# First four gate/up tile pairs by eight plain products on the first two token blocks; input loads and norm reordered

## The chip, the cores and the metric

The kernel runs on one core of one Trainium2 chip. TensorE (PE, with its weight loads PEld) does the matrix products, VectorE (DVE), ScalarE (ACT) and GpSimd (POOL) the elementwise work, and SyncE (SP) issues the DMAs. The metric is the device time of one execution in microseconds (us). TensorE's clock is granted at one of two levels, 1.2 or 2.4 GHz; the profile gives the granted share (1.00 is 2.4 GHz).

## The reference, cut to what matters

One decoder layer on 1104 token rows (16 meta rows, 1024 of the prompt, 64 of the samples) of width 1024, with a feed-forward block (FFN) ahead of the token mixers and one behind them:

```
x = x + 0.5*swiglu(rmsnorm(x, ffn1_norm), ffn1_w_gu, ffn1_w_down)
...                                   # input projection, four mixers, merge, output projection
x = x + 0.5*swiglu(rmsnorm(x, ffn2_norm), ffn2_w_gu, ffn2_w_down)
y = rmsnorm(x, final_norm)
def swiglu(x, w_gu, w_down):
    gate, up = split(x @ w_gu, 2, axis=-1)        # each 1104 x 2816
    return (silu(gate) * up) @ w_down
```

## The kernel before

Activations lie transposed: partitions are channels, columns are tokens. Each fp32 operand is split (`split`, L97 to L99) into a high part by an ACT cast and a low part by a DVE subtraction; a product of two split operands is three matmuls per 128 rows of depth.

**Gate and up** (`gate_up`, L411). The 2816 hidden columns are 22 tiles `f`. A pair is the gate tile and the up tile of one `f`. The tokens are four blocks of NS = 276; `p` = 0 is blocks 0 and 1, `p` = 1 is blocks 2 and 3. A pair on one `p` is a 2 by 2 by 2 block product (gate/up, two halves of the depth, two token blocks) done with seven products in place of eight (`steps`, L424). A product is 12 matmuls of 276 columns. The seven need sums of weight tiles (`a_prep`, L386: two raw tiles r1 and r2, a third raw tile s23, then casts) and sums of activation blocks, the factors B[p][0] to B[p][6] (`b_prep`, L363, with `factor`, L357). `two(0)` does `f` = 0 and 1 on `p` = 0; then `second()` loads the other half of the tokens and makes the factors of `p` = 1; `f` = 2 to 21 run on both `p`; `two(1)` does `f` = 0 and 1 on `p` = 1 at the end. The result goes by DMA to hS.

**Start of the first FFN** (`first`, `second`, `load_x`, L276). `load_x` loads row tiles of x (10 in all; 4, 2, 2 and 2 at a time), transposes them on TensorE (L67), copies them out with ACT (L309) and DVE (L307) in turn, takes the row sums of squares with ACT (L319) and DVE (L316) in turn, makes diagonal tiles on POOL (L326) and a matmul of them that spreads the norm over partitions (rs, L330). `scale` (L351) multiplies by norm and gain.

**Start of the second FFN.** `w_out` (the mixers' output projection) ends with the norm of each block; the same factors follow.

**Down** (`down`, L498). h is read back in groups of `f`: (2 to 5), (6 to 9), (10 to 13), (14 to 17), (18 to 21), then (0, 1). For each output tile `m` and token third `tb` (368 columns) a group adds into x by DVE (L511). The last group runs `tb` by `tb`, so that what follows a third, `norms` (L109) in the first FFN and `final` (L540) in the second, can begin beside the other thirds.

**Buffers that count.** wp holds 2 raw tiles and 3 each of whi and wlo; gw 2 raw tiles and 2 each; the pools up and v hold 8 and 6 slots. u22, block 3's second half (and its sums), lies in a raw tile of gw. The order on each engine is planned at build time: ready instructions go by priority, `high_priority` ahead of the rest, then by program order. Every DMA is issued by SP, in that order.

Of the kernel before, what the change touches and what calls it, by code (L numbers as in the profile page):

```python
# [7 lines left out]
F32 = mybir.dt.float32  # L8
# [5 lines left out]
D = 1024  # L14
DFF = 2816
# [27 lines left out]
class Kernel:  # L43
# [53 lines left out]
    def split(self, hi, lo, x):  # L97
        self.nc.scalar.copy(out=hi, in_=x)  # L98
        self.nc.vector.tensor_tensor(out=lo, in0=x, in1=hi.bitcast(F32), op=SUB)  # L99
# [176 lines left out]
    def load_x(self, half, xs):  # L276

        nc, I = self.nc, self.I
# [3 lines left out]
        blocks.append((I["x_sample"].rearrange("b t d -> (b t) d"), TS, TP))  # L282
        for pn, part in enumerate(((blocks[:4], blocks[4:6]), (blocks[6:8], blocks[8:]))[half]):
            ts = []
            for i, (src, r, c0) in enumerate(part):
                if i % 2 == 0:
                    pool = self.v if half and pn else self.up
                    xin = self.slot(pool, "xin", F32, (2, D))
                t = xin[:, i % 2]
                ld = nc.sync.dma_start(out=t[:r], in_=src).ins  # L290
                ts.append(t)
                if c0 == NMETA:
                    self.prm, self.po = self.gains()()
            self.after_x = ld
            for t, (src, r, c0) in zip(ts, part):
                for h in range(2):
                    ps = self.psum([128, 4, 128], "P" if h else "mm")
                    for j in range(4):
                        k = 4 * h + j
                        self.transpose(ps[:, j, :r], t[:r, k * 128:k * 128 + 128], r)  # L300
                    for b in range(c0 // NS, (c0 + r - 1) // NS + 1):
                        if b not in xs:
                            xs[b] = self.slot(self.v, "xs", F32, (8, NS))
                        lo, hi = max(c0, NS * b), min(c0 + r, NS * (b + 1))
                        dst, src = xs[b][:, 4 * h:4 * h + 4, lo - NS * b:hi - NS * b], ps[:, :, lo - c0:hi - c0]
                        if h:
                            nc.vector.tensor_copy(out=dst, in_=src)  # L307
                        else:
                            nc.scalar.copy(out=dst, in_=src)  # L309

            st = self.tp.tile([128, 3, 4], F32, tag="f_s", name="x_s")
            m, y, tmp = (st[:, i] for i in range(3))
            nc.gpsimd.memset(m, 0.0)
            for i, (t, (src, r, c0)) in enumerate(zip(ts, part)):
                if i % 2:
                    nc.vector.scalar_tensor_tensor(out=t[:r], in0=t[:r], scalar=1.0, in1=t[:r], op0=MULT, op1=MULT,  # L316
                                                   accum_out=m[:r, i:i + 1])
                else:
                    nc.scalar.activation(out=t[:r], in_=t[:r], func=AF.Square, accum_out=m[:r, i:i + 1])  # L319
            nc.vector.tensor_scalar(out=m, in0=m, scalar1=1.0 / D, scalar2=None, op0=MULT)  # L320
            self.rsqrt_rows(m, y, tmp)
            b0, n = part[0][2], 0
            ps = self.psum([128, 400], "P")
            for i, (src, r, c0) in enumerate(part):
                dg = self.tp.tile([128, 128], F32, tag="f_h", name="xdg")
                nc.gpsimd.tensor_scalar(out=dg[:r, :r], in0=self.ident[:r, :r], scalar1=y[:r, i:i + 1], scalar2=float(D),  # L326
                                        op0=MULT, op1=MULT)
                self.mm(ps[:, n:n + r], self.onesD[:r], dg[:r, :r])
                n += r
            nc.scalar.copy(out=self.rs[:, b0:b0 + n], in_=ps[:, :n])  # L330
        for b in (2 * half, 2 * half + 1):
            self.dq.dma_start(out=self.xS[:, :, NS * b:NS * (b + 1)], in_=xs[b])
# [24 lines left out]
    def factor(self, p, i, pool, x):  # L357

        t = self.slot(pool, f"b{p}{i}", F32R, (2, 4, NS))
        self.split(t[:, 0], t[:, 1], x)  # L360
        self.B[p][i] = t[:, 0], t[:, 1]

    def b_prep(self, p, u1, u2, u22, tmp, homes, first=0):  # L363


        tt = self.nc.vector.tensor_tensor
        b11, b21, b12, b22 = u1[:, 0:4], u1[:, 4:8], u2[:, 0:4], u22
        s3, s2 = tmp[:, 0:4], tmp[:, 4:8]
        if first == 0:
            self.factor(p, 0, homes[0], b11)  # L370
        self.factor(p, 1, homes[1], b21)
        tt(out=s3, in0=b22, in1=b12, op=SUB)
        tt(out=s2, in0=s3, in1=b11, op=ADD)
        tt(out=b12, in0=b12, in1=b11, op=SUB)
        self.factor(p, 2, homes[2], s2)
        self.nc.gpsimd.tensor_tensor(out=b21, in0=b21, in1=s2, op=SUB)
        self.factor(p, 4, homes[4], s3)
        if p:
            self.factor(p, 5, homes[5], b21)
            self.factor(p, 3, homes[3], b12)  # L380
        else:
            self.factor(p, 3, homes[3], b12)
            self.factor(p, 5, homes[5], b21)
        self.factor(p, 6, homes[6], b22)

    def a_prep(self, w, f):  # L386

        nc = self.nc
        with self.tc.high_priority() if f > 1 else ExitStack():
# [21 lines left out]
    def gate_up(self, w_in, first, second):  # L411
# [12 lines left out]
        def steps(f, A, p, q):  # L424
# [3 lines left out]
                 for c, pool, tag, n in (("a", self.ev, "e_a", 3), ("b", self.ev, "e_a", 3), ("c", self.tp, "f_s", 2),  # L428
# [42 lines left out]
        def two(p):  # L471
            run(*(steps(i, A, p, i) for i, A in enumerate([self.a_prep(w, i) for i in range(2)])))
        with self.tc.high_priority():
            first()
        two(0)
        second()
        for f in range(2, NF):
            a = self.a_prep(w, f)
            run(*(steps(f, a, p, p) for p in range(2)))
        yield  # L480
        two(1)

    GROUPS = [list(range(i, j)) for i, j in ((2, 6), (6, 10), (10, 14), (14, 18), (18, 22), (0, 2))]

    def load_h(self, fs):

        hs = []
        for f in fs:
            t = self.slot(self.v if fs == self.GROUPS[-1] else self.up, "h")
# [8 lines left out]
    def down(self, wd_in, start, hook=None, after=None):  # L498
# [6 lines left out]
        def out(hs, w, c0, m, tb):  # L505
            sl = slice(tb * NB, (tb + 1) * NB)
            o = m * 128 - c0
            ps = self.psum([128, NB])
            for i, (hh, hl) in enumerate(hs):
                self.mm3(ps, (w[0][:, i, o:o + 128], w[1][:, i, o:o + 128]), (hh[:, sl], hl[:, sl]), i == 0, i == len(hs) - 1)  # L510
# [4 lines left out]
        for gi, fs in enumerate(groups):  # L515
            hs = nxt
            cw = 1024 // len(fs)
            ws = []
            for c in range(1024 // cw):
# [1484 lines left out]
```

## Time and profile before

| what | before |
|---|---|
| median of 3 runs (2685.52 to 2690.02) | 2687.84 us |
| profiled execution | 2691.09 us |
| its span, first to last instruction | 2689.5 us |
| TensorE busy | 2528.3 us (94%), 17378 matmuls |
| VectorE busy | 1471.3 us (55%) |
| ScalarE busy | 913.8 us (34%) |
| mean granted clock | 0.968 |

The profiled execution is 1.6 us longer than its span and 3.25 us longer than the median. The busy shares are means over stages with different limits, so they say little of one stage; the windows of the section of rows below do.

### The profile page before, as it was taken

The page shows a single profiled execution, that of the slowest core. Times are in us where ns is not written, and L with a number is a line of the kernel's source. Part 1 is how long each engine was busy: PE and PEld are TensorE (multiplying, and loading weights), DVE is VectorE, ACT ScalarE, POOL GpSimd, SP SyncE. Part 2 cuts the span into 40 slices and gives each one's busy share as a digit, 9 for nine tenths or more (in the row PEclk, how much of TensorE's full clock was granted, in tenths as well). Part 3 has the DMA queues.
Part 4 walks back from the last instruction along what each step waited for, and adds up shares of the span by engine and source line. Part 5 has one row for each costly group of instructions (what it writes and reads, how often), then busy time and mean ns, then how long its engine had stood idle before and what let it go on. Part 6 is the DMA issues. An engine that isn't in the chain of part 4 may idle for free. (4 is left out here: it accounts for less than half of the span.)

```text
span 2689.5 us, 43298 instructions
## 1 busy us (share of the span) xinstructions
PE 2528.3 (94%) x17378; PEld 2452.0 (91%) x17378; DVE 1471.3 (55%) x2762; ACT 913.8 (34%) x1654; POOL 544.9 (20%) x595
## 2 busy tenths in 40 slices
PE   5599999999998988989999999999699999999997
PEld 5599999999997877978988999999699999999997
DVE  6644444556777448858653435343954444454535
ACT  4433333432204336324532313132433333341203
POOL 2122222200003003023452222212222222210000
PEclk7799999999998999989999999999899999999998
DMA  5222222453323232543443435332132222362311
GB/s 161 72 87 83 74 73 73 131 176 112 121 55 111 79 80 59 153 124 94 116 141 99 162 118 170 120 131 96 35 91 86 73 73 73 98 216 81 108 40 67
DMA packets 308997, 276.45 MB, mean 103 GB/s; under 512 B 62419, under 2 KB 266573, under 8 KB 308661
## 3 DMA queue, kind: packets, MB, share of 16 engines
q1 hardware_dynamic: 308797, 273.70, 32.9%
q8 instruction: 136, 2.23, 0.3%
q14 instruction: 64, 0.52, 0.1%
HBM read 192.11 MB, written 81.72 MB: 102 GB/s over the span
## 5 line engine op out<-in xcount | busy, mean ns | idle before, releaser
L59 PE MATMUL ps_mm<-u,whi 128*128 128x368 f32 (+1 forms) x2816 | 720.5, 337 | 11.4 <-DVE c_gl L144 4.7
L59 PE MATMUL ps_mm<-h,whi 128*128 128x368 f32 x2112 | 529.8, 332 | 3.3 <-DVE x L511 3.1
L59 PEld LDWEIGHTS ps_mm<-u,whi 128*128 128x128 f32 x2816 | 505.5, 191 | 26.9 <-issue 5.5
L98 ACT CAST whi<-raw 128x1024 fp32r<-128x1024 f32 (+1 forms) x303 | 297.7, 985 | 614.0 <-PE ps_mm L59 420.4
L59 PE MATMUL ps_mm<-u,wlo 128*128 128x368 f32 (+1 forms) x1408 | 471.7, 335 | 0.0
L59 PE MATMUL ps_mm<-b,whi 128*128 128x276 f32 x2816 | 446.8, 292 | 19.2 <-ACT b L98 10.0
L99 DVE TENSOR_TENSOR wlo<-raw,whi 128x1024 fp32r<-128x1024 f32 (+1 forms) x303 | 376.5, 1246 | 119.4 <-ACT whi L98 118.7
L59 PEld LDWEIGHTS ps_mm<-b,whi 128*128 128x128 f32 x2816 | 394.3, 190 | 21.5 <-ACT b L98 10.6
L59 PEld LDWEIGHTS ps_mm<-h,whi 128*128 128x128 f32 x2112 | 374.7, 188 | 6.6 <-DVE x L511 5.4
L59 PE MATMUL ps_mm<-h,wlo 128*128 128x368 f32 x1056 | 350.3, 332 | 0.0
L59 PEld LDWEIGHTS ps_mm<-u,wlo 128*128 128x128 f32 x1408 | 268.8, 191 | 4.2 <-issue 2.3
L511 DVE SCALAR_TENSOR_TENSOR x<-ps_mm,x 128x368 f32<-128x368 f32 x288 | 154.8, 539 | 187.3 <-PE ps_mm L59 185.8
L59 PE MATMUL ps_mm<-b,wlo 128*128 128x276 f32 x1408 | 237.5, 291 | 0.5 <-DVE wlo L99 0.5
L59 PEld LDWEIGHTS ps_mm<-b,wlo 128*128 128x128 f32 x1408 | 201.5, 189 | 0.8 <-DVE wlo L99 0.8
L59 PEld LDWEIGHTS ps_mm<-h,wlo 128*128 128x128 f32 x1056 | 198.4, 188 | 0.2
L401 POOL TENSOR_TENSOR raw<-raw 128x512 f32<-128x512 f32 x48 | 65.3, 1361 | 607.5 <-DVE wlo L99 570.4
L144 DVE TENSOR_TENSOR g_sg<-ps_mm,rs 128x368 f32<-128x368 f32 x96 | 51.8, 540 | 207.8 <-PE ps_mm L59 207.7
L59 PE MATMUL ps_vn<-b,whi 128*128 128x276 f32 x704 | 121.8, 294 | 36.5 <-ACT whi L98 36.5
L59 PEld LDWEIGHTS ps_vn<-b,whi 128*128 128x128 f32 x704 | 102.9, 192 | 37.0 <-ACT whi L98 36.9
L462 POOL TENSOR_TENSOR e_g<-e_g,e_u 128x276 f32<-128x276 f32 x88 | 105.3, 1197 | 109.6 <-ACT e_g L461 64.8
L439 DVE TENSOR_TENSOR e_g<-ps_pre,e_a 128x276 f32<-128x276 f32 x88 | 38.9, 442 | 156.5 <-DMA hS<-e_g 149.7
L59 PE MATMUL ps_o<-b,whi 128*128 128x276 f32 x704 | 120.1, 293 | 2.1 <-DVE e_u L452 2.1
(473 smaller groups left out, 3338.8 us busy)
## 6 DMA issues: line engine op xcount, KB each, us to landing
raw<-in_ffn_w_gu SPq DMA_DIRECT2D x96, 512.0 KB
raw<-in_w_in SPq DMA_DIRECT2D x50, 512.0 KB
hS<-e_g SPq DMA_DIRECT2D x88, 276.0 KB
h<-hS SPq DMA_DIRECT2D x44, 552.0 KB
raw<-in_ffn_w_down SPq DMA_DIRECT2D x44, 512.0 KB
x<-xS SPq DMA_DIRECT2D x24, 552.0 KB
mgS<-g_mg SPq DMA_DIRECT2D x24, 552.0 KB
g_b<-brS SPq DMA_DIRECT2D x16, 552.0 KB
```

Of the source, the lines that this page charges most:

```text
L59: self.last_mm = self.nc.tensor.matmul(out=out, lhsT=lhsT, rhs=rhs, start=start, stop=stop, **kw).ins
L98: self.nc.scalar.copy(out=hi, in_=x)
L99: self.nc.vector.tensor_tensor(out=lo, in0=x, in1=hi.bitcast(F32), op=SUB)
L144: self.last_dve = self.nc.vector.tensor_tensor(out=out, in0=ps, in1=r, op=MULT).ins
L401: nc.gpsimd.tensor_tensor(out=s23[:, k2], in0=r1[:, k1], in1=r2[:, k1], op=SUB)
L439: add(out=g[:, 0], in0=gam, in1=e["a"], op=ADD)
L462: nc.gpsimd.tensor_tensor(out=g[:, 1], in0=g[:, 1], in1=e["u"], op=MULT)
L511: nc.vector.scalar_tensor_tensor(out=x[:, m, sl], in0=ps, scalar=0.5, in1=x[:, m, sl], op0=MULT, op1=ADD)
```

## The change

The first four pairs (NP = 4) are no longer done by seven products on `p` = 0. `plain` does them by eight, one token block `t` at a time: on block 0 with B[0][0] and B[0][1] (the plain halves of that block), on block 1 with B[0][3] (the difference of the blocks' first halves, added to the kept sums e_a) and B[0][6] (block 1's second half); these are factors that the seven products use later. Their weights are only cast, not summed (`a_load`, `a_parts`). Pairs 0 and 1 run on block 0, then on block 1; pairs 2 and 3 likewise. `b_prep` is cut in two, `b_first` and `b_rest`. On `p` = 0 one subtraction of `b_rest` moves from DVE to POOL. `seven((0, 1), 1)` runs after `f` = 7, `seven((2, 3), 1)` at the end. In the first FFN all ten tiles of x are issued early, weights between them; `load_x` is cut into `load_x`, `turn_x` and `stats_x`; four tiles are copied out by ACT alone; all squares but one are on ACT; the diagonal tiles are made by ACT. The last group of `down` has three `f` in place of two, each with its own weight tile of 1024 columns.

```diff
+    def stats_x(self, ts, pool, tag):
...
+            if i == 1 and c0 < NS:
+                nc.vector.scalar_tensor_tensor(out=sq, in0=t[:r], scalar=1.0, in1=t[:r], op0=MULT, op1=MULT,
+                                               accum_out=m[:r, i:i + 1])
+            else:
+                nc.scalar.activation(out=sq, in_=t[:r], func=AF.Square, accum_out=m[:r, i:i + 1])
...
+            nc.scalar.activation(out=dg[:r, :r], in_=self.ident[:r, :r], func=AF.Copy, scale=y[:r, i:i + 1])
+            self.mm(ps[:, n:n + r], self.onesD[:r], dg[:r, :r])
...
-    def b_prep(self, p, u1, u2, u22, tmp, homes, first=0):
...
+    def b_first(self, p, u1, u2, u22, tmp, homes, skip=()):
+        for i, x in ((0, u1[:, 0:4]), (1, u1[:, 4:8])):
+            if i not in skip:
+                self.factor(p, i, homes[i], x)
+        self.nc.vector.tensor_tensor(out=tmp[:, 0:4], in0=u2[:, 0:4], in1=u1[:, 0:4], op=SUB)
+        self.factor(p, 3, homes[3], tmp[:, 0:4])
+        if p == 0:
+            self.factor(p, 6, homes[6], u22)
+    def b_rest(self, p, u1, u2, u22, tmp, homes):
+        b11, b21, b12 = u1[:, 0:4], u1[:, 4:8], u2[:, 0:4]
+        (self.nc.vector if p else self.nc.gpsimd).tensor_tensor(out=b12, in0=u22, in1=b12, op=SUB)
+        self.nc.vector.tensor_tensor(out=tmp[:, 4:8], in0=b12, in1=b11, op=ADD)
+        self.factor(p, 2, homes[2], tmp[:, 4:8])
+        self.nc.gpsimd.tensor_tensor(out=b21, in0=b21, in1=tmp[:, 4:8], op=SUB)
...
+    def a_load(self, w, f):
+        pool = (self.wp, self.gw)[f % 2]
+        rs = [self.raw([128, 8, 128], pool) for _ in range(2)]
...
+    def a_parts(self, f, rs):
+        pool, out = (self.wp, self.gw)[f % 2], []
+        for r in rs:
+            h, l = (pool.tile([128, 8, 128], F32R, tag=x, name=x, bufs=3 if pool is self.wp else None) for x in ("whi", "wlo"))
+            self.split(h, l, r)
...
+        def plain(f, A, t, ea):
+            B = self.B[0]
+            ps = [self.psum([128, NS], tag) for tag in ("mm", "pre")]
+            g = self.ev.tile([128, 2, NS], F32, tag="e_g", name="e_g")
+            for i in range(2):
+                product(ps[i], A[i][0], B[3 if t else 0], True)
...
+            for i in range(2):
+                product(ps[i], A[i][1], B[6 if t else 1], False)
...
+            self.dq.dma_start(out=self.hS[f, :, NS * t:NS * (t + 1)], in_=g[:, 0])
...
-        two(0)
-        second()
-        for f in range(2, NF):
+        with self.tc.high_priority():
+            raws = todo[0]()
+            A = [self.a_parts(f, raws[f]) for f in range(2)]
+        for f0 in range(0, self.NP, 2):
+            fs = (f0, f0 + 1)
+            if f0:
+                with self.tc.high_priority():
+                    A = [self.a_parts(f, self.a_load(w, f)) for f in fs]
...
+            for t in range(2):
+                for i, f in enumerate(fs):
+                    plain(f, A[i], t, ea[i])
+                if f0 == 0 and t == 0:
+                    with self.tc.high_priority():
+                        todo[1]()
+            for fn in todo[2 + f0:4 + f0]:
+                fn()
+        for f in range(self.NP, NF):
             a = self.a_prep(w, f)
             run(*(steps(f, a, p, p) for p in range(2)))
+            if f == self.NP + 3:
+                seven((0, 1), 1)
         yield
-        two(1)
+        seven((2, 3), 1)
-    GROUPS = [list(range(i, j)) for i, j in ((2, 6), (6, 10), (10, 14), (14, 18), (18, 22), (0, 2))]
+    NP = 4
+    GROUPS = [list(range(i, j)) for i, j in ((4, 8), (8, 12), (12, 16), (16, 19), (0, 4), (19, 22))]
...
+        ws = [self.weights(wd[:, f:f + 1], 1, 1024) for f in groups[-1]]
         for tb in range(3):
-            for w, c0, ms in ws:
-                for m in ms:
-                    out(hs, w, c0, m, tb)
+            for m in range(8):
+                out(nxt, [[t[:, 0, 128 * m:128 * m + 128] for t in w] for w in ws], m, tb)
...
+            def parts(a_load):                      # first FFN
+                def first():
+                    gains = self.gains()
+                    ts = self.load_x(range(4), [up, up])
+                    raws = {0: a_load(0)}
+                    us["ts"] = self.load_x(range(4, 6), [up])
+                    raws[1] = a_load(1)
+                    us["ts2"] = self.load_x(range(6, 10), [up, up])
+                    self.prm, self.po = gains()
+                    self.turn_x(ts, xs, [v] * 4, ("mm", "P"), True)
+                    self.stats_x(ts, up, "vn")
+                    us[0] = block(v, 0)
+                    for i in range(2):
+                        self.factor(0, i, up, us[0][:, 4 * i:4 * i + 4])
+                    return raws
+                def second():                       # block 1: tiles 4, 5, b_first(0)
...
+                def fourth():                       # tiles 6 to 9: turn_x, stats_x
...
+                def third():
+                    self.b_rest(0, us[0], us[1], us[1][:, 4:8], tmps[0], homes[0])
+                def fifth():
+                    u22 = self.raw([128, 4, NS], self.gw)
+                    for b in (2, 3):
+                        self.scale(lambda k: u22[:, k - 4] if b == 3 and k > 3 else xs[b][:, k], lambda k: xs[b][:, k], b)
+                    tmp = self.slot(v, "bt", F32, (8, NS))
+                    self.b_first(1, xs[2], xs[3], u22, tmp, homes[1])
+                    self.b_rest(1, xs[2], xs[3], u22, tmp, homes[1])
+                return first, second, fourth, third, fifth
...                                                 # second FFN: first, second, third, fourth alike, from x in SBUF
```

## Rows read from the trace of the kernel before

**Rows 1.** Windows: busy us (instructions) of PE, PEld, DVE, ACT, POOL; granted clock, DMA.
```profile
150.00:160.00 10.00, 10.00 (x81) 10.00 (x80) 5.29 (x8) 2.94 (x5) 3.85 (x4) 1.00 0.41 126
2430.00:2440.00 10.00, 10.00 (x61) 10.00 (x60) 3.85 (x6) 1.06 (x1) 0.00 (x0) 1.00 0.16 52
```

**Rows 2.** Windows again, of the factors' matmuls alone (tile b): PE busy comes first.
```profile
0.00:112.80 112.80, 35.47 (x216) 33.02 (x216) 22.38 (x14) 15.15 (x14) 0.74 0.38 120
1893.90:1950.50 56.60, 32.30 (x216) 30.32 (x216) 21.39 (x13) 12.96 (x12) 0.86 0.10 31
```

**Rows 3.** Timeline of PE: start, us, what, xcount [idle before, releaser].
```profile
27.60 1.27 PE L59 MATMUL ps_mm<-b,whi 128*128 128x276 f32 x4
112.82 1.29 PE L59 MATMUL ps_vn<-b,whi 128*128 128x276 f32 x4 [23.17 <-ACT whi L98]
1894.07 0.67 PE L59 MATMUL ps_mm<-b,whi 128*128 128x276 f32 x4
1950.80 1.29 PE L59 MATMUL ps_vn<-b,whi 128*128 128x276 f32 x4 [13.30 <-ACT whi L98]
```

**Rows 4.** Timeline of DVE and POOL ahead of the first FFN's restart.
```profile
96.28 3.44 POOL L376 TENSOR_TENSOR xs<-xs,bt 128x1104 f32<-128x1104 f32 x1 [7.70 <-ACT b L98]
97.28 4.83 DVE L99 TENSOR_TENSOR b<-bt,b 128x1104 fp32r<-128x1104 f32 x2
108.31 1.31 DVE L99 TENSOR_TENSOR b<-raw,b 128x1104 fp32r<-128x1104 f32 x1 [1.18 <-ACT b L98]
109.70 1.26 POOL L401 TENSOR_TENSOR raw<-raw 128x512 f32<-128x512 f32 x1 [9.98 <-DVE b L99]
```

**Rows 5.** Windows of DVE-bound stretches (columns as rows 1).
```profile
0.00:22.04 22.04, 11.19 (x49) 8.59 (x49) 8.74 (x19) 8.88 (x18) 6.41 (x14) 0.87 0.79 253
22.04:109.70 87.66, 43.40 (x268) 39.80 (x268) 66.90 (x98) 40.95 (x58) 16.33 (x14) 0.71 0.30 91
1893.90:1937.50 43.60, 32.93 (x221) 30.62 (x219) 43.56 (x58) 23.21 (x31) 15.90 (x5) 0.92 0.11 34
```

**Rows 6.** Timeline of the first norm of x: diagonal tiles, then scale.
```profile
15.90 0.74 POOL L326 TENSOR_SCALAR xdg<-ident,x_s 16x16 f32<-16x16 f32 x2 [14.49 <-DVE x_s L107]
22.04 3.42 DVE L354 SCALAR_TENSOR_TENSOR ub<-xs,prm,rs 128x276 f32<-128x276 f32 x8 [1.65 <-ACT rs L330]
```

**Rows 7.** Groups by line, 0 to 112.8: xcount | busy us, mean ns | idle before.
```profile
L99 DVE TENSOR_TENSOR wlo<-raw,whi 128x1024 fp32r<-128x1024 f32 x8 | 11.2, 1409 | 3.8 <-ACT whi L98 3.8
L98 ACT CAST b<-ub 128x1104 fp32r<-128x1104 f32 x5 | 5.4, 1110 | 0.5 <-POOL ub L376 0.5
L99 DVE TENSOR_TENSOR b<-ub,b 128x1104 fp32r<-128x1104 f32 x5 | 6.3, 1300 | 0.0
L316 DVE SCALAR_TENSOR_TENSOR xin<-xin 128x1024 f32<-128x1024 f32 x4 | 5.3, 1326 | 0.0
L307 DVE COPY xs<-ps_P 128x512 f32<-128x512 f32 x5 | 3.5, 691 | 7.8 <-PE ps_P L67 7.8
L403 DVE TENSOR_TENSOR raw<-raw 128x512 f32<-128x512 f32 x3 | 2.1, 686 | 0.1
```

**Rows 8.** Between the first FFN and the mixers: a window, PE's timeline.
```profile
810.10:850.70 40.60, 28.41 (x150) 24.75 (x148) 36.27 (x63) 27.44 (x53) 21.63 (x36) 0.90 0.37 129
...
846.25 1.60 PE L59 MATMUL ps_P<-raw,onesD 128*128 128x368 f32 x2 [6.70 <-DVE raw L132]
850.72 2.21 PE L59 MATMUL ps_mm<-u,whi 128*128 128x368 f32 x6 [2.87 <-ACT whi L98]
```

**Rows 9.** The end: a window, and DVE's wait for a raw tile.
```profile
2668.40:2689.50 21.10, 5.08 (x38) 3.85 (x36) 11.93 (x38) 10.98 (x29) 0.00 (x0) 0.66 0.41 143
...
2678.05 0.69 DVE L558 TENSOR_TENSOR raw<-ps_vn,fg 128x512 f32<-128x512 f32 x1 [1.32 <-DMA out_y_prompt<-raw]
```

**Rows 10.** PE's wait in `two(1)`, and SP's longest wait up to 120 us.
```profile
2388.30 0.77 PE L59 MATMUL ps_mm<-b,whi 128*128 128x276 f32 x4 [1.09 <-ACT e_b L444]
...
SPq L82 <- DVE wlo L99: 39.5, 3, 24.8
```

More of the change, by code (lines that the diff above doesn't have):

```diff
@@ L281, in load_x @@
             blocks.append((I["x_prompt"][0, 128 * i:128 * i + 128], 128, NMETA + 128 * i))
[L282 to L330, printed above, removed]
@@ L331, in load_x @@
-        for b in (2 * half, 2 * half + 1):
-            self.dq.dma_start(out=self.xS[:, :, NS * b:NS * (b + 1)], in_=xs[b])
+        return blocks + [(I["x_sample"].rearrange("b t d -> (b t) d"), TS, TP)]
+    def load_x(self, tiles, pools):
+        ts = []
+        for i, n in enumerate(tiles):
+            src, r, c0 = self.tokens()[n]
+            if i % 2 == 0:
+                xin = self.slot(pools[i // 2], "xin", F32, (2, D))
+            self.nc.sync.dma_start(out=xin[:r, i % 2], in_=src)
+            ts.append((xin[:, i % 2], r, c0))
+        return ts
@@ L409, in a_prep, with gate_up @@
         return [a11, a12, s2, s1, s3, a22, s4]
-    def gate_up(self, w_in, first, second):
+    def gate_up(self, w_in, parts):
         nc = self.nc
@@ L1861, in block @@
                 return u
-            def first():
-                self.load_x(0, xs)
-                u1, u2 = block(v, 0), block(v, 1)
-                self.b_prep(0, u1, u2, u2[:, 4:8], self.slot(v, "bt", F32, (8, NS)), [up] * 7)
-            def second():
-                self.load_x(1, xs)
-                u22 = self.raw([128, 4, NS], self.gw)
-                for b in (2, 3):
-                    self.scale(lambda k: u22[:, k - 4] if b == 3 and k > 3 else xs[b][:, k], lambda k: xs[b][:, k], b)
-                self.b_prep(1, xs[2], xs[3], u22, self.slot(v, "bt", F32, (8, NS)), [v, v, v, v, up, v, v])
+            tmps, us, homes = {}, {}, ([up] * 7, [v, v, up, v, v, v, v])
@@ L1874, in build @@
             es_cm = ExitStack()
             self.gkey, self.B = "ffn1_norm", ([None] * 7, [None] * 7)
-            with ffn(I["ffn1_w_gu"], I["ffn1_w_down"], first, second) as start:
+            with ffn(I["ffn1_w_gu"], I["ffn1_w_down"], parts) as start:
                 es_g.close()
@@ L1954, in build, with parts, first, second @@
             self.w_out(done)
[L1956 to L1966 removed]
+            def parts(a_load):
+                tmps, us = {}, {}
+                homes = [None] + [up] * 6, [v, v, v, v, up, v, up]
+                def first():
+                    raws = {0: a_load(0), 1: a_load(1)}
+                    self.factor(0, 1, up, ub[0][:, 4:8])
+                    return raws
+                def second():
+                    us[1] = block(up, 1, rows(1))
+                    tmps[0] = self.slot(up, "bt", F32, (8, NS))
+                    self.b_first(0, ub[0], us[1], us[1][:, 4:8], tmps[0], homes[0], (0, 1))
+                def third():
+                    self.b_rest(0, ub[0], us[1], us[1][:, 4:8], tmps[0], homes[0])
+                def fourth():
+                    u22 = self.raw([128, 4, NS], self.gw)
+                    u2, u3 = (self.slot(up, "ub", F32, (8, NS)) for _ in range(2))
+                    for u, b in ((u2, 2), (u3, 3)):
+                        self.scale(lambda k: u22[:, k - 4] if b == 3 and k > 3 else u[:, k], rows(b), b)
+                    tmp = self.slot(v, "bt", F32, (8, NS))
+                    self.b_first(1, u2, u3, u22, tmp, homes[1])
+                    self.b_rest(1, u2, u3, u22, tmp, homes[1])
+                return first, second, third, fourth
+            with ffn(I["ffn2_w_gu"], I["ffn2_w_down"], parts) as start:
                 es_g.close()
```

149 lines of the change are left out of this document (94 added, 55 removed).

## The prediction, made before the kernel was run

> **What bounds the kernel now.** I read the busy table first: TensorE is at 94%, no other engine above 55%. So the kernel is a stream of matmuls, and time can only come from matmuls added or from stretches where TensorE starves. The page's 40 slices show where: the first three, one near 835 us, one near 1940, and the last. I then took windows of 10 us. In the steady part TensorE is busy 10.00 of 10.00 us and does 81 matmuls of 276 columns or 61 of 368 in them, so 0.1235 and 0.164 us each [rows 1]; no other engine counts there. In the first FFN the first such product starts at 27.60, but by 112.8 only 216 have been done, 26.7 us of work; after that the stream has no gap [rows 2, 3]. In the second it is the same 216 from 1894.07 to the restart at 1950.80 [rows 2, 3]. Before both restarts TensorE stands 23.17 and 13.30 us "for ACT whi" [rows 3]. Read back, that is not ACT: the weights of `f` = 2 need a third raw tile (s23), the pool gw has two raw tiles, and u22 holds one until its last split, DVE's L99 from 108.31; POOL's L401 follows at 109.70 [rows 4]. So both starts end when DVE has finished **all** factors of all four blocks, and DVE is what sets it: busy 66.90 of 87.66 us in the first FFN, 43.56 of 43.60 in the second [rows 5].
>
> **The change part by part.**
>
> *Matmuls.* Four pairs by eight products are 4 x 8 x 12 = 384 matmuls, against 336 by seven: 48 more, 5.9 us per FFN, 11.9 us in all, always paid. The gain is that 384 can run before the seven-product factors exist. If T is the time of the restart, 216 were done by T before, and 384 - 48 = 336 worth of useful ones by T after. So each start gains (T before - T after) + 120 x 0.1235 = (T before - T after) + 14.8 us, provided TensorE finds time for all 384 (47.4 us) ahead of T.
>
> *First FFN, where TensorE can start.* Diagonal tiles on POOL take from 15.90 until the scale starts at 22.04 [rows 6]; on ACT, four of about 0.35 us, I put this at 19.3. Half a scale (1.7), one cast (1.11 [rows 7]): the first product at about 22.5, 5 us earlier than 27.60. Then 47.4 us, 3 us for the slow clock at the start (four matmuls span 1.29 us after a wait and 0.67 in the stream [rows 3]) and some 6 us of transposes and norms: the plain products can be over at 79. That is one bound of T.
>
> *First FFN, DVE.* T is still set by u22's last split, because `fifth` takes the same raw tile and `a_prep(4)` needs two. DVE was busy 8.7 + 66.9 us up to there [rows 5]. Off: four of five squares 5.1, four copies 2.7, the pair sums (L402, L403) of two pairs 2.7, about one cast's low part 1.4 (eight of 1.4, against eight and two halves), one subtraction moved to POOL 1.3 [rows 7], small ones 2. On: the moved subtraction runs on POOL, and beside POOL's 3.44 us the two DVE splits of 1.30 took 4.83 [rows 4], so 2.2. From 75.6 this leaves 62.6, of which some 8 lie ahead of 19.3. So 19.3 + 55 busy + 4 for the alternation of ACT and DVE in the last three splits (1.2 each, [rows 4]) + 6 of idling for data + 3.2 from the last split to the first product (109.62 to 112.82) gives T = 88. If DVE stays as idle as before (66.9 of 87.7, a share of 0.76) it is 95. Taken: 88, gain 112.8 - 88 + 14.8 = **39.6** (27 to 51, the upper end with T = 79 and no slow clock at the restart).
> The Trainium skill, "SBUF — State Buffer", section "SBUF: two separate sides", says that VectorE and GpSimd share one port pair as an exclusive lock, and the loser waits for the whole instruction. The rows agree (4.83 for 2.60 beside 3.44), and this speaks against the move to POOL: by the page it could cost the whole 3.44 us against 1.3 gained, and T would be 89 for 88.
>
> *Input loads.* They were issued as buffers came free; now all are issued at once, 6.4 MB with the weights of two pairs. The first chain doesn't wait longer: the three big tiles still go ahead of weights. ACT takes four squares, four copies and the diagonals more, some 10 us, on 50 busy of 110 [rows 5]; it is nearest to a bound in `fourth`, which I see end at about 50, when DVE is with `third`.
>
> *Second FFN.* DVE was full from 1893.9 to 1937.5 [rows 5]. One subtraction less (1.3), the POOL lock 2.2, pair sums 1.4 less, low parts of two more pairs less those sums' casts 1.7 more, evictions 0.9 more: 2 us more in all. T moves from 1950.8 to 1952; TensorE's own bound is 1894.1 + 47.4 = 1941.5. Gain 14.8 - 1.2 = **13.6** (6 to 27).
>
> *End of the first FFN's `down`.* The last group starts at 810.1 and needs 24 x 6 x 0.164 = 23.6 us, but the mixers' first product comes at 850.72, 40.6 us later: DVE is busy 36.27 of 40.60 with evictions and the norm, and TensorE waits 6.70 and 2.87 us at the end [rows 8]. With three `f` the group starts 11.8 us later and lasts 35.4. DVE's 36 us now run beside 35.4 of matmuls, not 23.6; the restart comes 38 to 41 us after the group's start, the gain is 11.8 plus 0 to 2.5. Against it: three wide weight tiles hold all three whi buffers until the last matmul, so the mixers' first cast (1.05) can't be early, and a raw tile held by the norm may put its load behind; that could take 8. Taken **12** (4 to 16).
>
> *End of the kernel.* 21.1 us pass after the last product, and in them DVE waits until 2678.05 for a raw tile that `final` of the second third still held [rows 9]. The last third's products now take 11.8 us for 7.9, so `final(1)` is up to 3.9 us further by then. Taken **3** (0 to 4).
>
> *Costs.* In each `down` the third whi buffer comes free only with the previous group's last product: a cast of 1.05 us less the six matmuls that run first, 0.75 each, 1.5. `seven((0, 1), 1)` stands inside the steady loop with seven products per weight preparation; its like cost TensorE 1.09 us in `two(1)` [rows 10]: 2.2 for two (0 to 8). More weights (4 MB), one more wide tile and eight more stores per FFN are hidden: DMA is at 0.16 to 0.41 in the steady windows [rows 1]. Where that cover fails, SP queues weights behind a store (see the rival).
>
> *Sum.* 39.6 + 13.6 + 12 + 3 - 1.5 - 2.2 = 64.5 us off the profiled execution, 2691.1 to 2626.6. That execution is 3.25 above the median of 2687.84, so the median goes to **2623**.
>
> **The rivals.**
> - *DVE doesn't get faster* (the plain pairs' casts and evictions have priority and push the factors back): T stays 112.8 and 1950.8. Each start then gains 14.8, the ends 15, the costs 3.7: 2687.8 - 40.9 = 2647 (2640 to 2660). For it: DVE is full in the second FFN. Against: 14 us leave DVE in the first.
> - *The ends give nothing* (whi and raw buffers hold the next stage back as before): 15 less, 2638.
> - *u22 doesn't block*: a free raw tile goes to `a_prep(4)` first, and TensorE runs through both starts. Gains 51, 27, 14 and 4 less 3.7: 2595. Against: before, u22 got it.
> - *Slower: SP's queue.* All DMAs stand in one order. A weight load that waits for a raw tile stops the stores of g behind it, g has two buffers, and `plain` stores twice per pair. SP's longest such wait was 24.8 us [rows 10], then beside an idle stretch. Three of these on TensorE's path cost 74 us and eat the gain of 64.5; with three it is 2697, from there slower. For it: eight stores instead of two in each start. Against: the planner places loads where buffers are free.
> - *It doesn't do what it says*: TensorE finds no room for the plain products ahead of T, and the 11.9 us of extra ones cancel what the ends give: 2685.
>
> **How the numbers follow.** Forecast 0.58 (own range 2606 to 2638), DVE no faster 0.18, ends give nothing 0.07, u22 free 0.09, slower 0.06, no change 0.02. The range of 8 in 10 runs from 2600 to 2655: it leaves out the slower case, no change, half of u22 free and a little of DVE. A change of 0.2% (5.4 us) is about what a measurement of this kernel can tell from none; by the cases faster by more has 0.92, within 0.02, slower 0.06.
>
> **What would show it.** Right: first product at about 22.5; restarts of the gapless stream at about 88 and, in its own time, some 58 us after the second FFN's first product, with 384 factor matmuls ahead of each; the mixers' first product 38 to 41 us after the last group's start; the end behind the last product near 18 us. Wrong: gaps between the plain products of over 10 us in a start (a factor or a weight late: DVE, or SP's order), a wait over 5 us after `f` = 7, or a third weight tile that stops the last group.

## The result, and the profile after

The changed kernel takes 2623.2 us (median of 4 executions, 2620.7 to 2625.3) against 2687.6 us: a ratio of 0.976 (95% interval 0.974 to 0.978), 64.4 us less. The forecast was 2623 us, 64.5 us less. The sum came out by luck as much as by its mechanism: several terms were missed by 5 us or more, and the misses cancelled.

Where the time went, from the two profiled executions (spans 2689.5 and 2621.0, 68.5 us apart):

| from | to | before | after | gain |
|---|---|---|---|---|
| start | mixers' first product | 850.72 | 806.64 | 44.1 |
| mixers' first product | second FFN's first product | 1043.35 | 1041.57 | 1.8 |
| second FFN's first product | end | 795.4 | 772.8 | 22.6 |

TensorE in the page's busy table, and the windows of the factors' matmuls alone (tile b; PE busy and count, clock, DMA share, GB/s), to set beside [rows 2]:

```profile
PE 2529.9 (97%) x17474; PEld 2457.5 (94%) x17474; DVE 1456.7 (56%) x2729; ACT 915.6 (35%) x1667; POOL 532.4 (20%) x578
...
0.00:96.30 96.30, 59.88 (x432) 0.89 0.55 168
1848.20:1910.00 61.80, 58.21 (x441) 0.97 0.24 73
```

Before, 216 stood ahead of each restart. PE's timeline of the changed kernel (start, us, what, xcount [idle before, releaser]), against [rows 3]:

```profile
14.58 1.09 PE L67 MATMUL ps_P<-ident,xin 128*128 128x128 f32 x4 [3.25 <-DMA xin<-in_x_prompt]
...
26.35 1.27 PE L59 MATMUL ps_mm<-b,whi 128*128 128x276 f32 x4
...
45.45 1.29 PE L59 MATMUL ps_mm<-b,whi 128*128 128x276 f32 x4 [3.15 <-ACT b L98]
96.35 1.29 PE L59 MATMUL ps_vn<-b,whi 128*128 128x276 f32 x4 [3.91 <-ACT whi L98]
...
1848.21 0.68 PE L59 MATMUL ps_mm<-b,whi 128*128 128x276 f32 x4
...
1882.86 1.29 PE L59 MATMUL ps_mm<-b,whi 128*128 128x276 f32 x8 [3.48 <-ACT whi L98]
...
1908.92 0.66 PE L59 MATMUL ps_vn<-b,whi 128*128 128x276 f32 x4
...
1920.92 0.77 PE L59 MATMUL ps_mm<-b,whi 128*128 128x276 f32 x4 [1.53 <-ACT e_b L471]
```

The idle time of 23.17 us ahead of the first restart is 3.91 now. That of 13.30 in the second FFN has no counterpart: the product that waited there now starts at 1908.92 without a wait. A wait of 3.48 inside the plain products is the longest left in that start; the 1.53 at 1920.92 lies inside pair 4. What releases the first restart is as it was [rows 4], 16.5 us earlier: u22's last split on DVE, then pair 4's difference on POOL, which waits for u22's raw tile:

```profile
91.84 1.31 DVE L99 TENSOR_TENSOR b<-raw,b 128x1104 fp32r<-128x1104 f32 x1 [0.38 <-ACT b L98]
...
93.23 1.26 POOL L427 TENSOR_TENSOR raw<-raw 128x512 f32<-128x512 f32 x1 [4.51 <-DVE b L99]
```

The last group of the first FFN's `down` (from 760.9, where the first of its 216 matmuls starts, to the mixers), then PE, SP and ACT there, against [rows 8]; last, the window behind the kernel's last product, against [rows 9]:

```profile
760.90:806.60 45.70, 38.92 (x220) 36.29 (x218) 43.47 (x104) 26.41 (x52) 16.13 (x17) 0.99 0.35 117
...
790.80 0.60 PE L59 MATMUL ps_mm<-h,whi 128*128 128x368 f32 x2 [1.71 <-DVE x L578]
806.64 2.21 PE L59 MATMUL ps_mm<-u,whi 128*128 128x368 f32 x6 [4.07 <-ACT whi L98]
...
801.26 0.38 SPq L82 DMA_DIRECT2D raw<-in_w_in  x1
...
805.55 1.04 ACT L98 CAST whi<-raw 128x1024 fp32r<-128x1024 f32 x1 [0.98 <-DMA raw<-in_w_in]
...
2603.70:2621.00 17.30, 3.43 (x29) 2.79 (x26) 9.28 (x29) 8.47 (x23) 0.00 (x0) 0.72 0.40 144
```

From the group's start to the mixers it takes 45.7 us, in which TensorE is busy 38.9; before, it was busy 28.4 of 40.6. The third `f` adds 11.8 us of matmuls and the stretch grew by 5.1, so 6.7 are gained. The norm's wait of 6.70 is gone, and what is left at the end is a weight load that was issued at 801.26. The end takes 17.3 us (before, from the last product at 2668.7, 20.8).

### The profile page after: what moved, and what is told of

The parts are those of the page before. It is cut to its first block, busy times and chain, and to the rows that moved or that the text cites. A ratio compares the mean times of both kernels' runs of the same rounds, so it can differ in the third digit from the quotient of the medians.

```text
span 2621.0 us, 43531 instructions
## 1 busy us (share of the span) xinstructions
PE 2529.9 (97%) x17474; PEld 2457.5 (94%) x17474; DVE 1456.7 (56%) x2729; ACT 915.6 (35%) x1667; POOL 532.4 (20%) x578
## 4 chain that ended last, share of the span: by engine, by line
PE 82%; DVE 7%; DMA 4%; ACT 3%; issue 2%; POOL 1%; SPq 1%; DVEq 0%; POOLq 0%; ACTq 0%
PE ps_mm L59 62%; PE ps_pre L59 7%; PE ps_vn L59 6%; PE ps_o L59 5%; DMA a_bc<-qsP 1%; PE ps_P L59 1%; DVE wlo L99 1%; PE ps_pre L67 0%; DVE b_t L1646 0%; DMA raw<-in_ffn_w_gu 0%; DVE b L99 0%; DVE d_acc L783 0%; DVE x L578 0%; DMA xin<-in_x_prompt 0%; ACT whi L98 0%
## 5 line engine op out<-in xcount | busy, mean ns | idle before, releaser
L98 ACT CAST whi<-raw 128x1024 fp32r<-128x1024 f32 (+2 forms) x305 | 299.7, 986 | 617.4 <-PE ps_mm L59 417.6
L99 DVE TENSOR_TENSOR wlo<-raw,whi 128x1024 fp32r<-128x1024 f32 (+2 forms) x305 | 384.2, 1263 | 109.0 <-ACT whi L98 108.1
L427 POOL TENSOR_TENSOR raw<-raw 128x512 f32<-128x512 f32 x44 | 57.3, 1303 | 520.0 <-DVE wlo L99 499.3
L59 PE MATMUL ps_pre<-b,whi 128*128 128x276 f32 x896 | 145.6, 291 | 0.0
L59 PEld LDWEIGHTS ps_pre<-b,whi 128*128 128x128 f32 x896 | 127.2, 191 | 0.0
L1802 ACT ACTIVATE g_sg<-g_sg 128x368 f32<-128x368 f32 x96 | 48.9, 509 | 198.4 <-DVE g_sg L144 198.4
L489 POOL TENSOR_TENSOR e_g<-e_g,e_u 128x276 f32<-128x276 f32 x80 | 99.3, 1241 | 76.7 <-issue 34.7
```

The lines of the kernel that those rows point to most:

```text
L59: self.last_mm = self.nc.tensor.matmul(out=out, lhsT=lhsT, rhs=rhs, start=start, stop=stop, **kw).ins
L99: (eng or self.nc.vector).tensor_tensor(out=lo, in0=x, in1=hi.bitcast(F32), op=SUB)
L427: nc.gpsimd.tensor_tensor(out=s23[:, k2], in0=r1[:, k1], in1=r2[:, k1], op=SUB)
L489: nc.gpsimd.tensor_tensor(out=g[:, 1], in0=g[:, 1], in1=e["u"], op=MULT)
L1802: self.last_act = nc.scalar.activation(out=sg, in_=sg, func=AF.Tanh, scale=0.5).ins
```

## The experiments

All are edits of the changed kernel, and their times are medians of 4 executions or more, beside runs of the kernel before on the same chip. The theory: both starts end when DVE has made all factors (u22's raw tile is the gate), the plain products fill TensorE until then, and the longer last group pays at both ends.

**How far one profile can be trusted.** The changed kernel once more:

> The changed kernel again, without an edit. In every run so far the stretch of the mixers, which no edit touches, took 1038 to 1042 us, longest in the changed kernel's own profile (806.64 to 1848.21, 1041.6), and the one-edit variants came out 2 to 5 us below what their own stretch explains. If that was scatter of the run in which the changed kernel was measured, it comes out at 2618 to 2621 us here, with a mixers' stretch of 1038 to 1040; if the edits themselves reach into the mixers, at 2622 to 2625 with 1041 to 1042.

The median is 2623.8 us (2615.9 to 2624.5), the ratio 0.9765 (0.975 to 0.978): the time stands, and the edits aren't measured against a stray value. But the execution that was profiled took 2615.9: restart at 95.82, mixers' first product at 805.72, mixers 1038.1 us, second FFN 770.4, with a wait of 0.3 in pair 4 where the first profile has 1.53. So two profiles of one kernel differ by 0.9 us up to the mixers, 3.5 in the mixers and 2.4 in the second FFN; below, differences of that size are called scatter. Neither of the two readings was right: the same kernel did both. Over its 9 executions the median is 2623.7, which is what the edits are compared with.

**Without the plain products** (`rest` is `fourth` and `fifth`; they stand behind `seven`, as their work did in the kernel before):

```
-        for f0 in range(0, self.NP, 2):
...
+            first()
+            second()
+            third()
+        seven((0, 1), 0)
+        for fn in rest:
+            fn()
-        for f in range(self.NP, NF):
+        for f in range(2, NF):
...
+        yield
+        seven((0, 1), 1)
```

> All of the change but the plain products: the reordered loads and norm, the new groups of down and their ends stay; pairs 0 and 1 go through the seven products as before, and pairs 2 and 3 in the loop. Theory (the gain of the starts is 384 products that run before the factors are done): the restart of the first FFN comes at 88 to 96 us, but with 216 factor products ahead of it where the changed kernel has 432, so the first start loses about 20 us; the second start falls back to the kernel before's 57 us from first product to restart and loses 15 to 19. Time 2652 to 2668 us. Rival (the reordering of loads and norm is what moved the first restart from 112.8, and the plain products add little): 2625 to 2640.

2684.6 us (ratio 0.9985, 0.998 to 0.9995): slower than either theory allowed. DVE's lighter work, the diagonals on ACT and the early loads are all in it, and yet the restart is back at 112.97, within 0.2 us of [rows 3]. PE and DVE show why, and the windows from the first scale to the end of u22's last split (DVE's busy time comes second) say how much DVE had to do, first in the changed kernel, then in this run:

```profile
70.07 0.66 PE L67 MATMUL ps_o<-ident,xin 128*128 128x128 f32 x4 [0.54 <-DVE e_g L487]
...
112.97 1.29 PE L59 MATMUL ps_vn<-b,whi 128*128 128x276 f32 x4 [18.84 <-ACT whi L98]
...
83.68 0.51 DVE L360 SCALAR_TENSOR_TENSOR xs<-xs,prm,rs 128x276 f32<-128x276 f32 x1 [1.70 <-ACT rs L338]
...
22.90:93.15 70.25, 55.42 (x79) 0.92 0.46 136
...
23.39:109.78 86.39, 54.68 (x76) 0.72 0.23 73
```

The last four input tiles are transposed at 70.07, behind the seven products on PE and their evictions; so the second pair of blocks is scaled only from 83.68, with DVE busy just 4.52 of the 20 us from 60 to 80. DVE has no more to do than in the changed kernel (54.7 us for 55.4), but it idles 31.7 us on the way and not 14.8; in the kernel before it worked 66.9 and idled 20.8 [rows 5]. The second FFN lost too: 62.5 us from its first product (1886.14) to its restart (1948.62), for 56.7 before, which eats much of what the ends bring; why, these runs don't show. For the first restart the next run tests the order of the norm.

**The same with the second norm first**, in the first FFN alone (`mid` is `fourth`, the transposes and the norm):

```
             first()
             second()
+        for fn in mid:
+            fn()
         third()
         seven((0, 1), 0)
```

> The run without plain products (e1_no_plain) again, but in the first FFN the transposes and the norm of the last four input tiles stand ahead of the seven products of pairs 0 and 1, as they do in the changed kernel; the second FFN is that of e1_no_plain. Theory (the first restart came back to 112.97 there because the factors of the second pair of blocks stood behind the seven products and their PSUM, not because VectorE had more to do: it was busy 33.6 of 60 us from 40 to 100): the restart comes at 97 to 104 us, and the time is 2670 to 2678 us. Rival (the sum of VectorE's work sets the restart, as the prediction had it): the restart stays at 111 to 114, the time at 2682 to 2687.

2664.5 us (ratio 0.991), under the theory's range; the restart is at 95.85:

```profile
43.09 0.46 PE L67 MATMUL ps_o<-ident,xin 64*128 64x64 f32 x4
...
95.85 1.29 PE L59 MATMUL ps_vn<-b,whi 128*128 128x276 f32 x4 [20.31 <-ACT whi L98]
...
64.02 5.09 DVE L360 SCALAR_TENSOR_TENSOR xs<-xs,prm,rs 128x276 f32<-128x276 f32 x12 [1.01 <-ACT rs L338]
...
23.08:92.66 69.58, 54.19 (x76) 0.75 0.29 91
```

The transposes end by 43.6, the scale starts 19.7 us earlier, the restart comes 17.1 earlier, and the mixers' first product 17.2 (846.74 to 829.57). DVE's work is the same (54.2 us), its idling falls from 31.7 to 15.4. So **it is the order of that norm that moves the first restart here**, not the plain products (95.85 without them, 96.35 with them), and a lighter DVE moves nothing without it. The new order under the old, heavier DVE was not run; by the next run it would have come later by about as much as DVE has more to do, so both are needed. What the plain products bring is this run against the changed kernel: 22.9 us at the mixers' first product, 23.0 from the second FFN's first product to the end (795.8 to 772.8), 40.8 by the medians (this profile is of the slowest of its four executions, 2669.0). Against the kernel before, the 23.0 is too much: without plain products the second start takes 61.5 us here, where it took 56.7 before.

**DVE's work, made longer:** four low parts of the second pair of blocks twice.

```
         self.split(t[:, 0], t[:, 1], x, eng)
+        if p and i in (0, 1, 3, 2):
+            self.nc.vector.tensor_tensor(out=t[:, 1], in0=x, in1=t[:, 0].bitcast(F32), op=SUB)
```

> The changed kernel with four low parts of the second pair of blocks' factors computed twice, 4 x 1.3 = 5.2 us more on VectorE ahead of u22's last split in each FFN; the result is the same. Theory (VectorE's work up to u22's last split sets the first restart, and in the second FFN TensorE still has work when it comes): the restart moves from 96.35 to 100 to 102, the second FFN loses 0 to 3 us; 2627 to 2632 us. Rival (a chain of waits with slack on VectorE sets the first restart): the restart moves by under 2 us; 2622 to 2625.

2630.1 us (2629.6 to 2630.9). u22's last split goes from 91.84 to 97.18, the restart from 96.35 to 101.68: 5.3 us for 5.2 of work.

```profile
97.18 1.31 DVE L99 TENSOR_TENSOR b<-raw,b 128x1104 fp32r<-128x1104 f32 x1 [1.18 <-ACT b L98]
...
101.68 1.29 PE L59 MATMUL ps_vn<-b,whi 128*128 128x276 f32 x4 [9.42 <-ACT whi L98]
```

So in the new order DVE does set the first restart. In the second FFN, whose stretch is 777.1 us for 772.8, a wait of 2.4 us appears at that place (PE's waits, `ps_vn` for `whi`): the slack there took in some 3 of the 5.2 us.

**u22's raw tile:**

```
-            r1, r2, s23 = (self.raw([128, 8, 128], pool) for pool in (None, self.gw, self.gw))
+            r1, r2, s23 = (self.raw([128, 8, 128], pool) for pool in (None, self.gw, None if f == self.NP else self.gw))
```

> For pair 4 alone the third raw tile (s23) is taken from the pool wp and not from gw, where u22 holds one of two. Theory (u22 in gw sets the first restart): GpSimd's difference for pair 4 no longer waits for the last split of u22 at 93 us, the gap of 3.9 us ahead of 96.35 and the slow clock behind it are gone, 3 to 7 us off; in the second FFN, where no gap stood at that place, nothing. 2616 to 2620 us. Rival (VectorE's sum of work sets it, whatever tile is free): pair 4's splits push the last factors back by as much and the gap moves by under 2 us; 2621 to 2625.

2615.9 us (2615.0 to 2617.1). POOL's difference for pair 4 no longer waits for u22, and TensorE has no gap near 96:

```profile
71.38 2.47 POOL L427 TENSOR_TENSOR raw<-raw 128x512 f32<-128x512 f32 x1 [5.38 <-DMA raw<-in_ffn_w_gu]
...
95.38 0.67 PE L59 MATMUL ps_vn<-b,whi 128*128 128x276 f32 x4
```

The mixers' first product comes at 800.96, 4.8 to 5.7 us earlier than in the two profiles of the changed kernel: the gap of 3.91, and the slow clock behind it (0.64 from 96.3 to 105 in the changed kernel, 1.00 here). The gate is u22's tile, as the prediction had it.

**The subtraction back on DVE:**

```
-        (self.nc.vector if p else self.nc.gpsimd).tensor_tensor(out=b12, in0=u22, in1=b12, op=SUB)
+        self.nc.vector.tensor_tensor(out=b12, in0=u22, in1=b12, op=SUB)
```

> The subtraction that the change moved to GpSimd (b12 of the first pair of blocks) is back on VectorE. Theory (GpSimd's instruction locks VectorE out for longer than the 1.3 us that it takes off it: in the changed kernel splits of 1.3 took 3.65 and a 0.17 us instruction 2.20 beside it): the factor products ahead of 45.4 us and the first restart come 1 to 3 us earlier, in the second FFN 0 to 1; 2619 to 2622 us. Rival (the move was worth what it takes off VectorE, 1.3 us in each FFN): 2624 to 2626.

2615.9 us (2615.1 to 2617.8), less than the theory allowed. DVE first in the changed kernel, beside POOL's instruction, then with the edit:

```profile
44.50 2.20 DVE L329 TENSOR_SCALAR x_s<-x_s 128x4 f32<-128x4 f32 x1 [0.47 <-ACT xin L328]
...
44.12 2.55 POOL L383 TENSOR_TENSOR ub<-ub 128x1104 f32<-128x1104 f32 x1 [22.62 <-DVE bt L375]
```

```profile
42.53 1.31 DVE L383 TENSOR_TENSOR ub<-ub 128x1104 f32<-128x1104 f32 x1
...
45.10 0.16 DVE L329 TENSOR_SCALAR x_s<-x_s 128x4 f32<-128x4 f32 x1
```

On POOL the subtraction took 2.55 us and held a DVE instruction of 0.16 until it was over. From the second block's scale to the last split of the first pair DVE needs 16.3 us with the subtraction (37.50 to 53.77) and 17.6 without it (39.04 to 56.61). The restart is at 94.33, 1.5 to 2.0 earlier, but 1.0 of that stands already at the first scale (21.87 for 22.90 and 22.82), ahead of the edit's place. The second FFN's wait of 3.48 is 0.86. The Trainium skill, "SBUF — State Buffer", section "SBUF: two separate sides", calls the port pair of the two engines an exclusive lock, held for a whole instruction; these rows agree. The gain of 7.8 us is more than these places show (0.5 to 1.0 at the first restart behind that head start; 1.3 to 3.7 in the second FFN, partly scatter).

**The end of the first FFN.** The norm's scratch out of the raw tile:

```
-            self.rsqrt_rows(ps, self.rs[:, sl], acc[0])
+            self.rsqrt_rows(ps, self.rs[:, sl], pool.tile([128, NB], F32, tag="f_h", name="n_t"))
```

> In the norm ahead of the mixers the scratch of the reciprocal root is a tile of its own and no longer the raw tile that holds the sum of squares. Theory (the weights of the mixers' first products stood behind that raw tile: freed at 801.2, load issued at 801.26, cast at 805.55, TensorE idle 4.07 us): the load is issued some 5 us earlier, the cast then waits only for the third whi buffer, free with the last product of down; the wait of 4.07 falls to 1 to 2, 2 to 3 us off; 2620 to 2621 us. Rival (the load stands behind the stores of x on SP's queue): the load still comes at about 801 and nothing changes, 2622 to 2624.

2615.0 us (2612.7 to 2616.2), more than expected. SP, ACT and PE:

```profile
794.69 0.38 SPq L82 DMA_DIRECT2D raw<-in_w_in  x1
...
801.64 1.03 ACT L98 CAST whi<-raw 128x1024 fp32r<-128x1024 f32 x1
...
802.72 1.28 PE L59 MATMUL ps_mm<-u,whi 128*128 128x368 f32 x6 [1.79 <-ACT whi L98]
```

The load goes out 6.6 us earlier and the wait of 4.07 is 1.79, so it was the raw tile and not SP's queue: 2.3 us at that place, 3.0 to 3.9 with the stream ahead of it. The rest of the 8.7 lies in the mixers and the second FFN, where nothing but scatter is to be seen.

**A last group of two again:** `(16, 20), (0, 4), (20, 22)` in GROUPS.

> Groups (4-7), (8-11), (12-15), (16-19), (0-3), (20, 21): the last group of both down has two pairs again where the change has three. Theory (a longer last group hides the norm's VectorE work and final): the mixers' first product comes 8 us later behind an otherwise equal stream, the end behind the last product goes from 17.4 back to some 21, and 1 to 3 us come back because two wide weights fit the three whi buffers; 2630 to 2635 us. Rival (the ends give nothing, the 12 us come from elsewhere): 2620 to 2625.

2627.2 us (2623.3 to 2630.8). The old stall is back:

```profile
810.05 1.60 PE L59 MATMUL ps_P<-raw,onesD 128*128 128x368 f32 x2 [6.68 <-DVE raw L132]
814.26 2.21 PE L59 MATMUL ps_mm<-u,whi 128*128 128x368 f32 x6 [2.62 <-ACT whi L98]
```

The mixers start 7.6 us later, the end behind the last product is 20.5 instead of 17.3. In the second FFN's stream 2.0 come back against the first profile (753.5 for 755.5 us from its first to its last product) and nothing against the second (753.1), so this is scatter; the changed kernel's profile shows no wait of TensorE for the third wide weight. By the traces the longer group is worth 8.8 us (7.6 + 3.2 - 2.0) or more, by the medians 3.5, and the interval of either ratio is some 4 us wide to each side: the places bear the theory out, the size stays open.

**SP's order in the second FFN:** the plain products' stores issued by POOL (`nc.gpsimd.dma_start` at L520).

> The stores of g in the plain products are issued by GpSimd and not from SP's queue. Theory (in the second FFN a weight load stood behind such a store on SP, and the cast behind that load cost TensorE 3.48 us and its clock): the wait at 1882.9 and the slow stretch behind it are gone, 3 to 5 us off; 2618 to 2621 us. Rival (the load waited for a free raw tile, not for the store): 2622 to 2625; and the descriptors written by GpSimd could hold up its subtractions and its products of g: up to 2630.

2618.3 us (2614.9 to 2621.2). The place doesn't confirm it. The cast no longer waits for its load (2.11 us in the changed kernel's profile), but TensorE's wait is still 2.6 us for 3.48, because the cast now follows an ACT instruction that itself waits for g's last store:

```profile
PE ps_mm L59 <- ACT whi L98: 2.6, 1, 2.6
...
1877.72 0.40 ACT L514 ACTIVATE e_g<-ps_mm 128x276 f32<-128x276 f32 x1 [0.63 <-DMA hS<-e_g]
1878.02 1.04 ACT L98 CAST whi<-raw 128x1024 fp32r<-128x1024 f32 x1
```

The unedited kernel had 2.8 there in its second profile. So taking the stores off SP's queue shortens that wait by little or nothing; DVE is busy 39.8 of the 40 us from 1845 to 1885 here. Where the 5 us of the median come from, no row shows.

**The gains' loads behind the first input tiles:**

```
-                    gains = self.gains()
                     ts = self.load_x(range(4), [up, up])
+                    gains = self.gains()
```

> The changed kernel with the three small loads of the norms' gains issued behind the first four input tiles, not ahead of them. Theory (those small loads stand ahead of the input on SP's queue: the first tile came at 6.01 us where the kernel before had it at 4.84, and the tile that TensorE then waited for at 14.58): the input comes about 1 us earlier and the first product at 24.8 to 25.6 instead of 26.35; the restart, which hangs on VectorE, follows by 0.5 to 1 us; 2621 to 2623 us. Rival (the first product hangs on the sixteen engines' rate, with weights and input in one stream, and not on the issue): the first product stays within 0.3 us of 26.35 and the time at 2623.

2617.4 us (2616.3 to 2620.4). The tile that came at 14.58 comes at 11.33:

```profile
11.33 0.66 PE L67 MATMUL ps_o<-ident,xin 128*128 128x128 f32 x4 [1.17 <-DMA xin<-in_x_prompt]
...
25.62 1.29 PE L59 MATMUL ps_mm<-b,whi 128*128 128x276 f32 x4 [1.60 <-ACT b L98]
...
92.82 0.78 PE L59 MATMUL ps_vn<-b,whi 128*128 128x276 f32 x4 [3.92 <-ACT whi L98]
...
23.51 1.05 ACT L98 CAST whi<-raw 128x1024 fp32r<-128x1024 f32 x1 [0.66 <-DMA raw<-in_ffn_w_gu]
24.46 1.11 ACT L98 CAST b<-ub 128x1104 fp32r<-128x1104 f32 x1
```

The small loads alone don't explain those 3.25 us: the order on SP changed further, with one weight load ahead of that tile where there were two. The first scale comes 2.2 us earlier (20.69 for 22.90), yet the first product gains only 0.7, the edge of the theory's range: ACT's cast of its factor stands behind the cast of a weight that waited for its load. But the restart gains 3.0 to 3.5: on DVE, which sets it, the second block's scale starts at 37.35 for 39.04 and the second pair's at 62.34 for 65.88.

**Three edits together** (u22, norm scratch, subtraction) **and five** (the gains' loads and POOL's stores too):

> Three edits together: the third raw tile of pair 4 from wp (e3_s23_else), the scratch of the norm's root in a tile of its own (e8_norm_tmp), and the subtraction back on VectorE (e9_sub_dve). Theory (three separate waits, the first restart, the second FFN's start and the mixers' start): with the gains in the stretches that their traces showed, 5.7 in the first FFN's start, 3.9 at its end, and 3.7 in the second FFN's start, 13 to 16 us off; 2606 to 2610 us. Rival (the first two of them overlap: without u22's gap the earlier restart of e9 brings nothing, and the rest is scatter of the mixers): 2610 to 2614.

> e10_three with the gains' loads behind the input (e5_gains_later) and the plain products' stores issued by GpSimd (e4b_store_pool). Theory: about 1 us from the loads and 1 to 2 from the stores, 2603 to 2608 us. Rival (with the subtraction on VectorE the second FFN's start no longer waits for those stores, and GpSimd's descriptors cost it time): as e10_three or up to 2 us slower.

2609.3 us (ratio 0.9708, 0.969 to 0.973) and 2610.0 us (0.9706): both are some 14 us below the changed kernel. The three come out in the theory's range. The second pair of edits adds nothing to them, as the rival of that run had it. Of the three edits' 14.4 us, 10.0 to 10.9 stand at the mixers' first product (795.71), where the same edits one by one gave 8.2 to 10.9 together. The rest was not where it was expected: the second FFN takes 774.6 us, no less than in the changed kernel; its wait for `whi` is down to 0.9, but waits for e_g and e_b (1.5 and 1.4) stand there instead.

## Why the prediction came out, point by point

- *Plain products, the "14.8".* **Mis-sized.** "384 - 48 = 336 worth of useful ones by T after" against "216" compares unlike counts: 48 of the 216 are pair 2's first products, which need only r1, and the same 48 (of pair 4) run ahead of T after. The windows say 432 and not 384. The term is 168 x 0.1235 = 20.7; the runs with and without plain products show 22.9 and 23.0 per FFN, the second with the reservation made there.
- *First restart, "T = 88".* **Failed in size and in reason.** It came at 96.35, above the bound of 95. The sum was the first scale at 19.3, 55 us of DVE's work, 4 + 6 of idling and 3.2 to the first product. Measured are 22.9, 55.4, 14.8 and 3.2: the work was right, but the scale came 3.6 us later and DVE idled 4.8 us more. The reason failed at the idling. The prediction laid T to DVE's sum of work and let the idling fall from 20.8 us to 10 without a cause for it (its bound of 95 alone kept the old busy share of 0.76; it is 0.79). In the kernel without plain products DVE has the lighter work, idles 31.7 us and the restart is at 112.97: what makes it idle is the order of the second norm's transposes, which stand behind the seven products on PE. The change moved them ahead, and the prediction had no term for that. That DVE sets T in the new order, and that u22's tile gates it, is shown.
- *First product, "22.5".* **Missed**: 26.35, since the first scale starts at 22.90 and not at 19.3. Diagonals on ACT were costed, the landing of the input was not: PE waits 3.25 us for a tile at 14.58. "Input loads: the first chain doesn't wait longer" fell with that; but where the tile comes at 11.33 the first product still comes at 25.62, behind a weight's cast on ACT.
- *First start together, "39.6".* T was 8.35 us late, the missing 48 are worth 5.9: 37.2. It is close because two errors cancel, which is luck.
- *The move to POOL.* The prediction put 2.2 on for 1.3 off, a loss of 0.9; the stretch shows a loss of 1.3 (17.6 for 16.3 us). Right in size. That the kernel without the move is 7.8 us faster is not explained by it.
- *Second FFN, "13.6", T = 1952.* **Too low.** It is 19 to 22 (22.6 and, in the second profile, 25.0 less the end's 3.5). T was not the limit there: u22's last split ends at 1904.6, and TensorE, with 432 matmuls behind it, comes to the one that would wait for u22's tile only at 1908.92, and doesn't wait. Its own stream was the limit, 60.7 us from its first product where the prediction put 47.4: 48 matmuls more (5.9), the wait of 3.48, and in the other 3.9 the clock behind that wait (0.83 from 1880 to 1890). By the start alone that is 20.7 - (60.7 - 56.7) = 16.7; which places give the rest, these runs don't show.
- *End of `down`, "12", 38 to 41 us.* **Mis-sized**: 45.7 us in both profiles, a gain of 6.7, inside its bounds of 4 to 16. The reserve that the prediction named (a raw tile held by the norm) is part of the reason: the run without it gives back 2.3 at the last wait, and inside the group TensorE waits another 2.6 us for evictions on DVE.
- *End of the kernel, "3", "near 18".* **Right**: 17.3, a gain of 3.5.
- *Third whi buffer 1.5, seven((0, 1), 1) 2.2.* **Too high**: TensorE shows no wait for the third weight at the start of the last groups (only 0.31 and 0.29 us for an eviction on DVE), and where the products of seven((0, 1), 1) run in the second FFN (from about 1990, behind 384 + 4 x 168 others) neither profile shows a wait.
- *The sum.* The first start was put 2.4 us too high and `down` 5.3; against that, the second FFN was put 5 to 8 too low and the costs 3 too high. That the medians fit the total to 0.1 us is luck: the two profiled executions differ by 68.4.
- *Rivals.* DVE no faster: half of it was true, since a lighter DVE moved nothing by itself. u22 doesn't block: it does in the first FFN, it doesn't count in the second. SP's queue: no wait that could be put down to it was over 3.5 us.

## What to carry to other kernels

Before you price a stall by the busiest engine's sum, undo the order around it: an in-order engine (here PE, with the second norm's transposes behind products that wait for factors) can hold the chain while the busy engine idles. In the sum for a restart, the engine's idling needs a cause as much as its work does. When two restarts are compared, count the same kind of useful work on both sides, with what runs ahead in either. And after the first gain look for the tile that gates the next: three one-line edits of buffers and engines gave 14 us more, of which 10 to 11 stand ahead of the mixers, where the traces had named the waits.

## What the runs showed of the hardware

One and the same program, profiled twice, was 7 us apart with no single place for it (0.9, 3.5 and 2.4 us in three stretches). A DVE instruction of four elements per partition took 2.20 us beside a POOL instruction and 0.16 without. Several one-edit kernels came out 2 to 6 us below what their own place explains; what does that stays open.
